# Sample keys and sequence 0's keys loaded in the prompt phase, output projection one sequence sooner

## Chip, cores and metric

The kernel runs on one core of a Trainium2 chip. The metric is the device time of the whole program in microseconds (us), the median over several runs. The engines are named as the profile names them: PE is TensorE's matmul (PEld its weight load), DVE is VectorE, ACT is ScalarE, POOL is GpSimd, SP is SyncE, which here only issues DMAs (SPq in the rows).

## What is computed

Two layers are run for two groups of tokens: one new stream of 1024 frames ("prompt") and 16 new frames for each of 8 running streams ("sample", 128 rows), which attend to 1024 cached keys and values each. Cut to the layer that the change touches:

```python
def _attn_gmlp_layer(x, cache_k, cache_v, ...):
    z = einsum('btd,de->bte', rmsnorm(x, norm_g), w_in)
    q, k, v, g_a, u_b, v_b, g_b = split(z)
    k_all, v_all = concat(cache_k, k), concat(cache_v, v)      # sample group only
    o = diff_attn(q, k_all, v_all, ...)                        # softmax(1) - lam * softmax(2), times v
    out_a = rmsnorm(o, subln_g) * 0.8 * silu(g_a)
    out_b = gelu(u_b) * spatial_gate(layernorm(gelu(v_b))) * silu(g_b)
    return x + einsum('bte,ed->btd', concat([out_a, out_b]), w_out)   # the output projection
```

Layer 1 is a convolution module (`w_in1`, a depthwise convolution of 31 taps, `w_out1`) on the normed result; then follows a last RMSNorm. Everything is float32 to the outside.

## The kernel before

**Precision and tiles.** A float32 product is made of three matmuls of split operands, high times high, high times low, low times high (`mm3`, L150). So every weight and every key that comes from memory goes through a split: a DMA into a tile named `raw`, a copy to the high part on ACT, a subtraction for the low part on DVE. Weights do this in `split_w` (L127). Keys are first transposed on PE into PSUM, and split from there (`kt_split`, L412). All of these `raw` tiles come from one pool of three buffers of 512 KB (`rawp`, L218): input weights, cached keys, the rows for the output projection and reloaded normed rows follow one another through the same three buffers.

Tokens come in 9 tiles of 128 rows: tiles 0 to 7 are the prompt, tile 8 is the sample group.

**Order of the work.** The program is written as one long sequence; a planner with a cost model then orders the instructions of each engine, an earlier place in the program being a higher priority, and hands out the buffers as it goes. An instruction whose inputs and buffer are there can so be put well before its place in the program. At run time each engine takes its instructions, and SP and POOL their DMAs, in the planned order.

**Prompt phase** (`phase_prompt`, L421). A loop over 32 steps n (4 heads, 8 query blocks) does attention, and beside it 45 gating "pieces" (`ga_piece`, `gm_piece`), three for every two steps. The last pieces belong to channel group 3. When all pieces are issued in program order (n = 30), `decode_begin` (L650) opens the pools of the decode phase, and the steps that are left, and the code after the loop, take from a list `ahead`: `setup` (loads the sample group's own keys and values, L673 to L678), and `keys_part(0, (i,))` for the four quarters of sequence 0's cached keys. A quarter is a `raw` load of two key tiles of 128, eight transposes in two groups of four, and the splits.

**Decode phase** (`phase_decode`, L712). A loop over the 8 sequences b; each issues `dscores(b)`, the keys of sequence b + 1 in two halves (`keys_part`), `dvalues(b - 1)` (cached values, loaded by POOL) and `dweights(b)`. Between them stand:

- `wl(b, j)`, which loads the next parts of `w_out0` as the table `WL` says: eight parts of 512 KB, four for each half of the output's columns;
- `prep(t)`: a `raw` tile (called cat below) is filled with the attention and the gating rows of tile t (`s_oa`, `s_ob`, two DMAs), transposed in two halves and split;
- `main(t)`: the output projection of tile t, 2 x 24 matmuls of 512 columns, the residual add, and the norm of layer 1. For t below `DIR` the normed rows are stored to `s_yn` and read back later; for the others they stay on chip.

Before, `prep` and `main` of tile b - 2 stand beside sequence b, so tiles 0 to 5 lie within the loop. After the loop come `dvalues(7)`, `prep(6)`, `dfinish` (norms the attention of the sample group and stores it to `s_oa`), `main(6)`, `prep(7)`, and then the hand-over to layer 1: `ynorm(t)` reloads normed rows through a `raw` buffer, and `yt` transposes and splits them; `main(7)`, `prep(8)` and `main(8)` stand among these. `prep(8)` reads what `dfinish` stored.

**Convolution phase** (`phase_conv`, L917). It starts with `split_w` of `w_in1`, through `raw` again; its first matmuls need token tiles 0 to 2 alone.

Of the kernel before, what the change touches and what calls it, by code (L numbers as in the profile page):

```python
# [11 lines left out]
F32 = mybir.dt.float32  # L12
# [7 lines left out]
P = 128  # L20
# [64 lines left out]
NSPLIT = True  # L85
MID = 1
ORDER = (0, 7, 1, 6, 2, 5, 3, 4)
DIR = 6
LOWG = ()
HP = 100  # L90
AHEAD = True
WL = ((0, 0, 2, 2), (2, 0, 2, 0))
VMID = False
TOEP = (2, 3, 4, 5)
TAIL = 1
# [7 lines left out]
class Builder:  # L103
# [317 lines left out]
    def phase_prompt(self):  # L421
        nc, tc, a = self.nc, self.tc, self.a
        w = a["w_in0"]
        with ExitStack() as st:
# [181 lines left out]
            def piece():  # L606
                nonlocal done
                if done < len(pieces):
                    pieces[done]()
                    done += 1  # L610

            for n, (h, qb) in enumerate((h, qb) for h in range(H) for qb in (order if h < H - 1 else LAST)):
                need = max(n + 2, round((n + 1) * LEAD)) if n < 8 else round((n + 1) * LEAD)
                need = min(need, len(pieces))
                while done < need - MID:
                    piece()
                if done == len(pieces) and not ahead and AHEAD:
                    while gates:
                        gate()
                    self.xstack.close()  # L620
                    ahead = self.decode_begin()
                elif ahead:
                    ahead.pop(0)()
                with tc.high_priority(offset=HP):
                    if n % 8 == 0:
                        head(h)
                    sc = scores(h, qb)
                    next(sc)
                    if VMID and pend is not None:
                        values(*pend)  # L630
                while done < need:
                    piece()
                with tc.high_priority(offset=HP):
                    new = next(sc)
                    if not VMID and pend is not None:
                        values(*pend)
                pend = new
# [9 lines left out]
            while ahead:  # L647
                ahead.pop(0)()

    def decode_begin(self):  # L650
        nc, tc, a = self.nc, self.tc, self.a
        dec = ExitStack()
        E = dec.enter_context
        vp = E(tc.tile_pool(name="vp", bufs=2, side="right", reuse_waits="tile"))
        ktp = E(tc.tile_pool(name="ktp", bufs=5, side="right", reuse_waits="tile"))
        ep = E(tc.tile_pool(name="ep", bufs=2, side="right", reuse_waits="tile"))
        ptc = E(tc.tile_pool(name="ptc", bufs=2, space=PSUM, side="right", reuse_waits="tile"))
        kTs = [ep.tile([P, H, P], F32R, name=f"kts{i}", bufs=1) for i in range(2)]
        vs = [ep.tile([P, 512], F32R, name=f"vs{i}", bufs=1) for i in range(2)]
        qs = [ep.tile([P, H, P], F32R, name=f"qs{i}", bufs=1) for i in range(2)]  # L660
        oacc = ep.tile([P, 512], F32, name="oacc", bufs=1)
        mk = ep.tile([P, C_SGN - C_FOLD], F32, name="mk", bufs=1)
        fold, own, place = mk[:, :64], mk[:, 64:576], mk[:, 576:]
        bs0 = ep.tile([P, 144], F32, name="bs0", bufs=1)
        seqs = [{} for _ in range(NB)]

        def setup():
            nc.sync.dma_start(out=mk, in_=a["cst"][:, C_FOLD:C_SGN])
            for c in range(2):
                nc.sync.dma_start(out=bs0[c * 64:(c + 1) * 64, :], in_=self.skew[:, :NQ, :144])  # L670
            nc.sync.dma_start(out=qs[0].bitcast(F32), in_=self.s_qh[:, :, T:])
            nc.sync.dma_start(out=qs[1].bitcast(F32), in_=self.s_ql[:, :, T:])
            raw = self.rawp.tile([P, 1024], F32, name="raw")  # L673
            nc.sync.dma_start(out=raw[:, :512], in_=self.k0s)
            nc.sync.dma_start(out=raw[:, 512:], in_=self.v0s)
            self.kt_split(raw[:, :512], kTs[0], kTs[1], ptc)
            nc.scalar.copy(vs[0], raw[:, 512:])
            nc.vector.tensor_tensor(vs[1], raw[:, 512:], vs[0].bitcast(F32), ALU.subtract)  # L678

        qz = [ep.tile([P, 2, 576], F32R, name=f"qz{i}", bufs=1) for i in range(2)]  # L680

        def keys_part(b, parts):
            if b >= NB:
                return
            K = seqs[b].setdefault("K", [])
            ck_ = a["cache_k0"][b].rearrange("(t p) h e -> p t (h e)", p=P)
            bq = slice(b * NQ, (b + 1) * NQ)
            if 0 in parts:
                if b < 2:
                    nc.gpsimd.memset(qz[b].bitcast(F32), 0.0)  # L690
                for i in range(2):
                    qv = qz[b % 2][:, i].rearrange("p (h s) -> p h s", s=144)
                    for c in range(2):
                        rs = slice(c * 64, (c + 1) * 64)
                        nc.gpsimd.tensor_copy(qv[rs, :, c * 64:c * 64 + NQ], qs[i][rs, :, bq].bitcast(F32))
            for i in parts:
                kr = self.rawp.tile([P, 1024], F32, name="raw").rearrange("p (t c) -> p t c", t=2)
                nc.sync.dma_start(out=kr, in_=ck_[:, 2 * i:2 * i + 2])
                KTh, KTl = [ktp.tile([P, H, 272 if i == 3 else 256], F32R, name=f"KT{n}x" if i == 3 else f"KT{n}",
                                     bufs=1 if i == 3 else 4) for n in "hl"]  # L700
                for j in range(2):
                    sl = slice(j * P, (j + 1) * P)
                    self.kt_split(kr[:, j], KTh[:, :, sl], KTl[:, :, sl], ptc)
                if i == 3:
                    nc.gpsimd.tensor_copy(KTh[:, :, 256:], kTs[0][:, :, bq].bitcast(F32))
                    nc.gpsimd.tensor_copy(KTl[:, :, 256:], kTs[1][:, :, bq].bitcast(F32))
                K.append((KTh, KTl))

        self.dec = dec, ep, vp, ptc, vs, oacc, fold, own, place, bs0, seqs, keys_part, qz
        return [setup] + [lambda i=i: keys_part(0, (i,)) for i in range(4)]  # L710

    def phase_decode(self):  # L712
# [114 lines left out]
        def prep(t):  # L827
            if t >= NT:
                return
            ts_ = slice(t * P, (t + 1) * P)  # L830
            cat = self.rawp.tile([P, D], F32, name="raw")
            nc.sync.dma_start(out=cat[:, :512], in_=self.s_oa[ts_, :])
            nc.sync.dma_start(out=cat[:, 512:], in_=self.s_ob[ts_, :])
            x = ck.tile([P, D], F32, name="xr", bufs=2)
            nc.sync.dma_start(out=x, in_=self.xrow(t))
            ch = ck.tile([P, 8, P], F32R, name="ch")
            cl = ck.tile([P, 8, P], F32R, name="cl")
            self.transpose_split(cat, [ch[:, :4], ch[:, 4:]], [cl[:, :4], cl[:, 4:]])
            st_[t] = (x, ch, cl)

        def main(t):
            x, ch, cl = st_[t]
            for i in range(2):
                ps = po_.tile([P, 512], F32, name="out")
                self.mm3(ps, [(ch[:, k], cl[:, k]) for k in range(8)], wb[i])
                xs = x[:, i * 512:(i + 1) * 512]
                nc.vector.tensor_tensor(xs, xs, ps, ALU.add)  # L847
            nc.gpsimd.dma_start(out=self.s_y1[t * P:(t + 1) * P, :], in_=x)
            xs = ck.tile([P, D], F32, name="yn")
            self.norm(xs, x, self.gb, NSPLIT and t < 8)  # L850
            if t < DIR:
                nc.gpsimd.dma_start(out=self.s_yn[t * P:(t + 1) * P, :], in_=xs)
            return xs
# [2 lines left out]
        nc.sync.dma_start(out=self.gb, in_=a["norm_g1"].partition_broadcast(P))  # L856
        for b in range(NB):
            dscores(b)
            if b > 1:
                prep(b - 2)  # L860
            keys_part(b + 1, (0, 1))
            wl(b, 0)
            if b > 0:
                dvalues(b - 1)
            wl(b, 1)
            if b > 1:
                main(b - 2)
            keys_part(b + 1, (2, 3))
            wl(b, 2)
            dweights(b)  # L870
            wl(b, 3)
        dvalues(NB - 1)
        prep(6)
        dfinish()
        m6 = main(6)
        prep(7)
        dec.close()
        self.pstack = ExitStack()
        self.ptr = self.pstack.enter_context(tc.tile_pool(name="ptr2", bufs=2, space=PSUM, side="right", reuse_waits="tile"))
# [16 lines left out]
            nc.sync.dma_start(out=yr, in_=self.s_yn[t * P:(t + 1) * P, :])  # L896
            yt(t, yr)

        ynorm(0)
        ynorm(1)  # L900
        yt(6, m6)
        m7 = main(7)
        prep(8)
        ynorm(2)
        ynorm(3)
        ynorm(4)
        ynorm(5)
        yt(7, m7)
        m8 = main(8)
        yt(8, m8)  # L910
# [305 lines left out]
```

## Time and profile before

| what | value |
|---|---|
| median of 3 runs | 1260.4 us (1257.78 to 1263.14) |
| the profiled execution | 1257.52 us, its span 1255.7 us |
| PE busy | 1186.4 us, 94% of the span |
| DVE, ACT, POOL busy | 830.0, 477.6, 365.6 us |
| granted clock, mean | 0.981 |
| DMA moved | 153.26 MB, 122 GB/s on the mean |
| first matmul of the output projection | 558.47 us |
| first matmul of the convolution phase | 770.33 us |

The profile's page gives the busy time of each engine, then the span in 40 slices, then the chain of work that ended last. Other views give stretches of time (busy time of each engine, granted clock, DMA rate) and the instructions of one engine in order of time: start, duration, engine, line, operation, output tile <- input tiles, and in brackets how long the engine had been idle and what ended that. A row with SPq is the issue of a DMA, not its transfer.

### The profile page before, as it was taken

To read this page: it belongs to the slowest core of one execution; us is meant where nothing else is said; L and a number is where in the kernel's file an instruction comes from. 1 tells how busy PE (TensorE), PEld (TensorE's weight loads), DVE (VectorE), ACT (ScalarE), POOL (GpSimd) and SP (SyncE) were. 2 spreads that over 40 slices of the span, in tenths; PEclk is the share of its full clock that TensorE was granted. 3 is DMA by queue.
4 is the path that set the end of the run, shared out by engine and by line. 5 is a ranking of instruction groups with operands and counts; after the bars stand their busy time and mean duration, and the time that the engine had idled before them with its cause. 6 is when DMAs were issued, how large, how long until landed. Compare 5 with 4: busy or idle time off the path is not lost.

```text
span 1255.7 us, 18564 instructions
## 1 busy us (share of the span) xinstructions
PE 1186.4 (94%) x6644; PEld 1078.1 (86%) x6644; DVE 830.0 (66%) x1695; ACT 477.6 (38%) x1090; POOL 365.6 (29%) x540
## 2 busy tenths in 40 slices
PE   6999999999989997889999999999999987999997
PEld 5878998999989887778888878999999987997886
DVE  5420225788687878686666535799999999267843
ACT  4431223445454545574544434211121212156421
POOL 2223223435353426222222221211424220033200
PEclk9999999999989999899999999999999997999999
DMA  8352444414141315685666545213231310212222
GB/s 295 106 164 70 152 150 128 119 55 116 39 124 42 112 41 163 225 287 203 223 213 232 185 150 184 66 40 88 72 108 49 122 59 24 67 35 101 101 96 73
DMA packets 121924, 153.26 MB, mean 122 GB/s; under 512 B 13577, under 2 KB 85281, under 8 KB 121824
## 3 DMA queue, kind: packets, MB, share of 16 engines
q1 hardware_dynamic: 107848, 108.21, 27.9%
q0 software_dynamic: 13840, 43.60, 10.2%
q8 instruction: 53, 0.87, 0.3%
q14 instruction: 39, 0.32, 0.1%
q10 hardware_dynamic: 144, 0.26, 0.1%
HBM read 116.22 MB, written 36.26 MB: 121 GB/s over the span
## 4 chain that ended last, share of the span: by engine, by line
PE 77%; DMA 8%; DVE 6%; ACT 4%; issue 2%; POOL 2%; SPq 0%; DVEq 0%; POOLq 0%; ACTq 0%
PE mm L155 50%; PE out L155 8%; PE py L1175 3%; PE S L155 3%; PE pa L589 2%; PE tr L416 2%; DMA vraw<-in_cache_v 2%; PE tr L165 2%; PE S L546 1%; PE S L547 1%; PE mm L787 1%; PE mm L761 1%; PE mm L786 1%; PE tr L584 1%; DVE wl L144 1%
## 5 line engine op out<-in xcount | busy, mean ns | idle before, releaser
L155 PE MATMUL mm<-yh,wh 128*128 128x384 f32 x576 | 196.5, 341 | 15.1 <-ACT sg L1024 12.6
L155 PE MATMUL mm<-yl,wh 128*128 128x384 f32 x576 | 195.2, 339 | 0.0
L155 PE MATMUL mm<-yh,wl 128*128 128x384 f32 x576 | 194.8, 339 | 0.0
L155 PE MATMUL mm<-wh,xh 128*128 128x384 f32 (+1 forms) x504 | 185.4, 369 | 1.3 <-DVE sg L469 0.6
L155 PE MATMUL mm<-wl,xh 128*128 128x384 f32 (+1 forms) x504 | 184.3, 366 | 1.7 <-DVE wl L144 1.7
L1151 DVE SCALAR_TENSOR_TENSOR acc<-u,cc,acc 128x1024 f32<-128x1024 f32 x145 | 185.4, 1279 | 0.4
L155 PE MATMUL mm<-wh,xl 128*128 128x384 f32 (+1 forms) x504 | 183.5, 364 | 0.0
L144 DVE TENSOR_TENSOR wl<-raw,wh 128x1024 fp32r<-128x1024 f32 (+1 forms) x72 | 91.3, 1274 | 91.6 <-ACT wh L143 91.0
L155 PEld LDWEIGHTS mm<-yh,wh 128*128 128x128 f32 x576 | 109.0, 189 | 15.9 <-ACT sg L1024 12.9
L155 PEld LDWEIGHTS mm<-yl,wh 128*128 128x128 f32 x576 | 109.1, 189 | 0.3
L155 PEld LDWEIGHTS mm<-yh,wl 128*128 128x128 f32 x576 | 109.0, 189 | 0.1
L155 PEld LDWEIGHTS mm<-wh,xh 128*128 128x128 f32 x504 | 95.5, 190 | 12.6 <-issue 1.1
L155 PEld LDWEIGHTS mm<-wl,xh 128*128 128x128 f32 x504 | 95.7, 190 | 11.7 <-DVE wl L144 3.2
L155 PEld LDWEIGHTS mm<-wh,xl 128*128 128x128 f32 x504 | 95.5, 190 | 8.8 <-DVE xl L168 0.3
L143 ACT CAST wh<-raw 128x1024 fp32r<-128x1024 f32 (+1 forms) x72 | 71.6, 1003 | 68.3 <-PE mm L155 30.6
L124 POOL TENSOR_TENSOR rr<-pw,mhalf 128x1 f32<-128x1 f32 x59 | 34.6, 586 | 169.2 <-DVE pw L123 160.8
L560 ACT ACTIVATE e<-S,nm 128x512 f32<-128x512 f32 (+5 forms) x96 | 55.2, 579 | 49.8 <-DVE nm L555 34.5
L1169 POOL TENSOR_TENSOR tw<-wx,same 128x640 f32<-128x640 f32 x24 | 37.4, 1560 | 80.3 <-PE py L1175 70.9
L552 DVE TENSOR_REDUCE nm<-S 128x1 f32<-128x512 f32 (+5 forms) x96 | 52.4, 550 | 12.1 <-PE S L547 11.4
L155 PE MATMUL out<-wh,cl 128*128 128x512 f32 x144 | 59.7, 415 | 0.0
L155 PE MATMUL out<-wh,ch 128*128 128x512 f32 x144 | 57.7, 401 | 1.7 <-DVE xr L847 1.2
L155 PE MATMUL mm<-wl,ch 128*128 128x512 f32 x144 | 56.9, 395 | 2.3 <-DVE wl L144 2.2
(287 smaller groups left out, 2572.7 us busy)
## 6 DMA issues: line engine op xcount, KB each, us to landing
raw<-in_cache_k SPq DMA_DIRECT2D x32, 512.0 KB, 4.5
vraw<-in_cache_v POOLq DMA_DIRECT2D x32, 512.0 KB, 5.2
raw<-in_w_in SPq DMA_DIRECT2D x24, 512.0 KB, 5.1
raw<-in_w_out SPq DMA_DIRECT2D x16, 512.0 KB, 4.1
raw<-in_w_in SPq DMA_DIRECT2D x32, 256.0 KB, 3.6
raw<-in_w_in SPq DMA_DIRECT2D x48, 128.0 KB, 3.2
s_y<-xr POOLq DMA_DIRECT2D x9, 512.0 KB, 5.5
x<-s_y SPq DMA_DIRECT2D x9, 512.0 KB, 4.1
```

The costliest lines, as they stand in the source:

```text
L124: m = nc.gpsimd.tensor_tensor(out, v[:, :w], self.mhalf[:, :w], ALU.pow)
L143: nc.scalar.copy(h[:, :ks * n], raw[:, :ks * n])
L144: (low or nc.vector).tensor_tensor(l[:, :ks * n], raw[:, :ks * n], h[:, :ks * n].bitcast(F32), ALU.subtract)
L155: m = self.nc.tensor.matmul(out, lhsT=x, rhs=y, start=(i == 0), stop=(i == n - 1))
L165: nc.tensor.transpose(ps[:, k * P:(k + 1) * P], src[:, kk * P:(kk + 1) * P], self.ident)
L416: nc.tensor.transpose(ps[:, h * P:(h + 1) * P], src[:, h * P:(h + 1) * P], self.ident)
L552: nc.vector.tensor_reduce(nm[:, j:j + 1], s[:, :n], AX.X, ALU.max, negate=True)
L560: nc.scalar.activation(e[:, j * n:(j + 1) * n], S[j][:, :n], AF.Exp, bias=nv, accum_out=zz[:, j:j + 1])
L589: nc.tensor.matmul(po, lhsT=wT[:, k * P:(k + 1) * P], rhs=hd["v"][:, k, :], start=(k == 0), stop=(k == qb))
L1151: tap = nc.vector.scalar_tensor_tensor(cv[:, :T] if k == CONV - 1 else acc, u[:, k:k + T], w1, acc, ALU.mult, ALU.add)
L1169: nc.gpsimd.tensor_tensor(tw.rearrange("p s (c f) -> p s c f", f=8), wx[:, g, :].rearrange("p (s f) -> p s f", f=8).unsqueeze(2).broadcast ...
L1175: nc.tensor.matmul(py, lhsT=tw[:, 4 - s, :], rhs=X[:, g, s:s + 176], start=(s == 0), stop=(s == 4))
```

## The change

Two things change in the order of the program; no arithmetic is added or removed.

1. `prefetch`, called in step n = 27 of the prompt loop, takes the three `raw` tiles for the sample keys and values and for the first two quarters of sequence 0's keys, and issues their four DMAs there. `setup` and `keys_part(0, ...)` use these tiles.
2. `prep(b - 1)` and `main(b - 1)` stand beside sequence b, so tiles 0 to 6 lie within the loop. Tile 6's normed rows now go through `s_yn` (`DIR` = 7). `WL` is changed so that all eight parts of `w_out0` are asked for before `main(0)`: two of them now stand between the two halves of sequence 1's keys, and none after sequence 2's first half. After the loop: `dvalues(7)`, `prep(7)`, `dfinish`, `main(7)`, `prep(8)`, seven reloads instead of six, `yt(7)`, `main(8)`, `yt(8)`.

```diff
-DIR = 6
+DIR = 7
+PRE = 27
-WL = ((0, 0, 2, 2), (2, 0, 2, 0))
+WL = ((0, 2, 2, 2), (2, 0, 0, 0))
...
+                if n == PRE:
+                    self.prefetch()
...
+    def keys_load(self, b, i):
+        kr = self.rawp.tile([P, 1024], F32, name="raw").rearrange("p (t c) -> p t c", t=2)
+        src = self.a["cache_k0"][b].rearrange("(t p) h e -> p t (h e)", p=P)
+        self.nc.sync.dma_start(out=kr, in_=src[:, 2 * i:2 * i + 2])
+        return kr
+
+    def prefetch(self):
+        raw = self.rawp.tile([P, 1024], F32, name="raw")
+        self.nc.sync.dma_start(out=raw[:, :512], in_=self.k0s)
+        self.nc.sync.dma_start(out=raw[:, 512:], in_=self.v0s)
+        self.fetched = raw, [self.keys_load(0, i) for i in range(2)]
...
-            raw = self.rawp.tile([P, 1024], F32, name="raw")
-            nc.sync.dma_start(out=raw[:, :512], in_=self.k0s)
-            nc.sync.dma_start(out=raw[:, 512:], in_=self.v0s)
+            raw = self.fetched[0]
...
-                kr = self.rawp.tile([P, 1024], F32, name="raw").rearrange("p (t c) -> p t c", t=2)
-                nc.sync.dma_start(out=kr, in_=ck_[:, 2 * i:2 * i + 2])
+                kr = self.fetched[1][i] if b == 0 and i < 2 else self.keys_load(b, i)
...
             dscores(b)
-            if b > 1:
-                prep(b - 2)
+            if b > 0:
+                prep(b - 1)
             keys_part(b + 1, (0, 1))
             wl(b, 0)
             if b > 0:
                 dvalues(b - 1)
             wl(b, 1)
-            if b > 1:
-                main(b - 2)
+            if b > 0:
+                main(b - 1)
             keys_part(b + 1, (2, 3))
             wl(b, 2)
             dweights(b)
             wl(b, 3)
         dvalues(NB - 1)
-        prep(6)
+        prep(7)
         dfinish()
-        m6 = main(6)
-        prep(7)
+        m7 = main(7)
+        prep(8)
...
-        ynorm(0)
-        ynorm(1)
-        yt(6, m6)
-        m7 = main(7)
-        prep(8)
-        ynorm(2)
-        ynorm(3)
-        ynorm(4)
-        ynorm(5)
+        for t in range(7):
+            ynorm(t)
         yt(7, m7)
         m8 = main(8)
         yt(8, m8)
```

More of the change, by code (lines that the diff above doesn't have):

```diff
@@ L685, in keys_part @@
             K = seqs[b].setdefault("K", [])
-            ck_ = a["cache_k0"][b].rearrange("(t p) h e -> p t (h e)", p=P)
             bq = slice(b * NQ, (b + 1) * NQ)
```

## The prediction

> **What bounds the kernel now.** I read the page first (busy times, the 40 slices, the chain), then the stretches of time around the decode phase, then SP's and PE's rows there.
>
> ```profile
> span 1255.7 us, 18564 instructions
> PE 1186.4 (94%) x6644; PEld 1078.1 (86%) x6644; DVE 830.0 (66%) x1695; ACT 477.6 (38%) x1090; POOL 365.6 (29%) x540
> ...
> PE   6999999999989997889999999999999987999997
> PEclk9999999999989999899999999999999997999999
> ...
> PE 77%; DMA 8%; DVE 6%; ACT 4%; issue 2%; POOL 2%; SPq 0%; DVEq 0%; POOLq 0%; ACTq 0%
> ```
>
> PE is busy for 94% of the span and carries 77% of the chain. No matmul is added or removed, so the time can only move by what changes in PE's idle time and in its clock. Slices 14 to 18 (440 to 565 us) and 23 to 25 (720 to 785) hold what the change can reach; there the stretches say (columns: length, busy us of PE, PEld, DVE, ACT, POOL with instructions, granted clock, DMA share, GB/s):
>
> ```profile
> 485.00:489.00 4.00, 1.10 (x6) 0.57 (x6) 3.53 (x12) 2.72 (x9) 4.00 (x7) 1.00 0.24 71
> 494.00:498.00 4.00, 0.72 (x4) 0.53 (x4) 3.20 (x7) 3.28 (x10) 3.95 (x5) 0.95 0.61 149
> 498.00:502.00 4.00, 3.94 (x17) 3.66 (x18) 3.85 (x12) 1.67 (x6) 1.14 (x3) 0.50 0.96 356
> 518.00:521.00 3.00, 0.64 (x6) 0.42 (x5) 1.92 (x3) 2.02 (x3) 2.25 (x6) 1.00 1.00 373
> 521.00:525.00 4.00, 2.73 (x13) 2.12 (x14) 3.45 (x8) 2.81 (x9) 0.00 (x0) 0.56 0.66 223
> 525.00:529.00 4.00, 4.00 (x23) 4.00 (x23) 2.46 (x5) 2.78 (x6) 0.00 (x0) 0.58 0.21 77
> 533.00:540.00 7.00, 6.54 (x42) 5.15 (x41) 5.98 (x11) 5.32 (x8) 2.11 (x8) 1.00 0.78 271
> 540.00:550.00 10.00, 8.67 (x61) 7.28 (x59) 8.44 (x13) 7.96 (x18) 2.22 (x5) 1.00 0.90 285
> 550.00:560.00 10.00, 8.47 (x49) 6.41 (x50) 8.87 (x13) 5.36 (x8) 1.61 (x3) 1.00 0.89 302
> 670.00:700.00 30.00, 30.00 (x189) 25.89 (x188) 19.80 (x30) 15.74 (x30) 9.03 (x13) 1.00 0.65 218
> 735.90:742.00 6.10, 4.86 (x21) 3.25 (x20) 3.06 (x8) 3.62 (x12) 1.97 (x3) 1.00 0.21 86
> 742.00:752.00 10.00, 10.00 (x57) 8.43 (x55) 4.04 (x8) 3.37 (x6) 3.13 (x3) 1.00 0.51 171
> 752.00:756.00 4.00, 2.26 (x13) 1.27 (x11) 2.58 (x5) 3.09 (x7) 1.15 (x2) 1.00 0.46 178
> ```
>
> Beside sequences with an output projection PE is full (30.00 of 30 us at 670): an output tile that leaves or enters such a stage only shifts work. Beside the first two sequences, 518 to 560, PE is idle for 2.36 + 1.27 + 0.46 + 1.33 + 1.53 = 6.95 us, and at 521 to 529 its clock is 0.56 to 0.58, which costs about 2.73 x 0.44 + 4 x 0.42 = 2.9 us more. So 9.8 us is all that can be won there. Behind the last sequence, 742 to 752, PE is full; what fills it is looked at below.
>
> **Part 1, the prefetch: nothing.** It moves four DMAs in the program, but the planner had them early already:
>
> ```profile
> 415.26 0.38 SPq L674 DMA_DIRECT2D raw<-out_k0s  x1
> 415.70 0.46 SPq L675 DMA_DIRECT2D raw<-out_v0s  x1
> 421.13 0.39 SPq L698 DMA_DIRECT2D raw<-in_cache_k  x1
> 436.65 0.39 SPq L698 DMA_DIRECT2D raw<-in_cache_k  x1
> ...
> 488.87 1.06 PE L416 MATMUL tr<-cst,raw 128*128 128x128 f32 x8 [2.90 <-issue]
> ```
>
> Sample keys and values and the two quarters of sequence 0 are issued at 415 to 437, in all three `raw` buffers, and first transposed at 488.87. PE's 2.90 us before that isn't theirs: the data has been there for some 45 us. By the code the new PSUM pool takes the place of the gating pieces' pool, and the last of these (DVE L469) ends at 488.8. That wait stays. The same three buffers are held, by the same tiles. From below: no gain, as nothing waits for these loads. From above: four issues of 0.4 us on SP ahead of the attention's own small loads, 1.7 us if those were late. I take 0; the cover is those 45 us.
>
> **Part 2, first sequences: a gain of about 5 us.** The unit that moves:
>
> ```profile
> 687.37 5.45 PE out L155 x24
> ...
> 741.73 1.03 PE L165 MATMUL tr<-cst,raw 128*128 128x128 f32 x8
> ```
>
> One tile is 2 x 5.45 + 1.03 = 11.9 us of PE. `main(0)` now stands beside sequence 1. Can it start sooner? It needs all of `w_out0` and its own cat tile through three `raw` buffers:
>
> ```profile
> 508.32 0.37 SPq L698 DMA_DIRECT2D raw<-in_cache_k  x1
> ...
> L137 SPq DMA_DIRECT2D raw<-in_w_out x8: 368/373/411, 512.8 to 547.1; - x8
> ...
> 518.01 1.05 ACT L143 CAST wh<-raw 128x1024 fp32r<-128x1024 f32 x1 [5.44 <-DMA raw<-in_w_out]
> 518.96 1.07 ACT L418 CAST KTh<-tr 128x512 fp32r<-128x512 f32 x2
> ...
> 520.97 1.78 PE L416 MATMUL tr<-cst,raw 128*128 128x128 f32 x8 [2.36 <-DVE KTl L419]
> ...
> 558.47 0.41 PE L155 MATMUL out<-wh,ch 128*128 128x512 f32 x1
> ```
>
> Between the first and the last weight part stand four key loads (the tables `WL` and `keys_part`): 11 steps in 34.3 us, 3.1 us a step. In the new order the first part takes the place of sequence 1's third key quarter, at 508.3; the last part is 12 steps on, at 545.5, only 1.6 us sooner than 547.1. But the first half's parts (5 steps, 523.8) and the cat tile (8 steps, 533.1) are there early: landed and split some 7 us later, the first 24 matmuls can run from about 540. They can fill the 1.33 + 1.53 us idle from 540 to 560: 3 us won. The second half starts about when it did.
>
> The other loss, 518 to 529, is a wait in ACT's queue: ACT stood 5.44 us for the first weight part, and the casts of sequence 1's second key quarter (518.96) were behind it; PE then had no keys to go on with. With the first part 4.5 us sooner, this wait shrinks by as much and may go: up to 3.6 us idle and 2.9 us of clock. What is late next is sequence 1's third and fourth key quarter, now two steps, 6.2 us, later, and the second weight part's cast stands ahead of theirs in ACT's queue: a wait of the same kind, down to -3 us (half of this one). No row shows the new order; I take +2, in the middle, as it is the same wait with another load in it. Together 5, ends 0 (3 - 3) and 9.5 (3 + 6.5), just under the 9.8 there is.
>
> **Part 3, behind the last sequence: a loss of about 8 us.** The tail's chain is `dfinish`, a store, a load, tile 8's transposes:
>
> ```profile
> 735.89 1.02 PE L793 MATMUL mm<-om,mk 128*128 128x512 f32 x2
> ...
> 743.08 0.60 POOL L812 DMA_DIRECT2D s_oa<-vraw  x1 [0.96 <-DVE vraw L810]
> ...
> 748.17 0.32 SPq L832 DMA_DIRECT2D raw<-s_oa  x1
> 748.60 11.79 SPq L896 DMA_DIRECT2D raw<-s_yn  x4
> 763.26 8.27 SPq L137 DMA_DIRECT2D raw<-in_w_in  x6
> ...
> raw<-s_oa SPq DMA_DIRECT2D x2, 256.0 KB, 3.2
> ```
>
> From sequence 7's last matmul (735.89) to the landing of tile 8's rows (748.17 + 3.2 = 751.4) pass 15.5 us, and SP's reloads of normed rows (748.60) are queued behind that load. Until 742 PE ends the tile in hand; then `main(7)` filled 742 to 752. With everything one tile sooner, the tile in hand is `main(7)`, and after 742 PE has only the transposes of two reloaded tiles and of tile 7, at most 3 x 1.03 = 3.1 us, for 9.4 us: 6.3 us idle. In return the 1.74 us idle of 752 to 756 shrinks, as the way is free for tile 8: 5 us net, 4.6 to 6.3.
>
> To this come the clock and the ring. After 2.9 and 3.28 us idle the clock was 0.50 at 498, after 3.6 us it was 0.56 to 0.58 for 8 us: 1.7 to 2.9 us lost each time. I take 2, and 0 as the lower end. [...]
>
> Tile 6 is now one store of 0.6 us on POOL, which nothing waits for, and one more reload in the ring ahead of `w_in1`, whose first load at 763.26 served matmuls that began at 770.33. With one step of 3.1 us as the upper end and 0 as the lower, as with less on PE the buffers come free sooner, I take 1. Sum of the tail: 5 + 2 + 1 = 8, ends 3 (3 us of idle if two more reloads get ahead of the waiting load and no slow clock) and 12.3 (6.3 + 2.9 + 3.1).
>
> **Sum.** 0 - 5 + 8 = +3 us. On the profiled execution, 1257.5 us (span 1255.7), that is 1260.5; this one lies 2.9 us under the median of 1260.4, so the forecast is 1263 us. The ends: -9.5 + 3 = -6.5, and 0 + 12.3 = +12.3. Half a per cent, 6.3 us, is about what a measurement of this kernel can tell from no change; the forecast is no change.
>
> **Rivals.**
>
> *Slower.* Sequence 1's late key quarters make PE stand a second time near 525 to 535. For it: ACT takes its casts in order, and from 518 to 525 the DMA share is 0.66 to 1.00. Against: by the pace the fourth quarter is issued at 517.6 and landed by 523, and PE wanted it only at 533. It decides from about 10 us of delay on. Price: the 3 us of fill are lost again, and the tail's 8 us stand alone: +8, 1268 us; with the tail's upper end +12, 1272 us.
>
> *Faster.* The stall of 518 to 529 goes altogether (-9.5), and the planner puts reloads three and four ahead of tile 8's load, so that the tail costs its lower end of 3: -6.5 us, 1254 us. For it: the 5.44 us wait hangs on one load that comes 4.5 us sooner. Against: DMA is as full, and before, the reloads were queued behind that load though their buffer was free.
>
> *It doesn't do what it says.* The planner holds `main(0)` back to where the last weight part lands, as now, and the tile only moves by name: no fill, but then tile 7 is also left over for the tail, and both terms go: 1260 us. This lies within no change.
>
> **Chances.** Forecast 0.45 and the empty change 0.10, both within 0.5%; slower 0.28 and faster 0.17 beyond it. The range, 1253 to 1272, runs from the faster case's price to the slower one's and leaves out about one in ten at each end.
>
> **What would show it.** Part 1: first key transposes again at about 489 after some 2.9 us of idle. Part 2: first projection matmul at about 540, less than 7 us idle from 518 to 560; ACT's wait for the first weight part below 2 us. Part 3: after the last sequence one idle stretch of 4 to 7 us ending in DMA `raw<-s_oa` or the transposes of tile 8, a clock below 0.7 behind it, and the stages between as full as now. It is wrong if PE stays full in the tail, or if sequence 1's scores wait for keys.

## The result, and the profile after

| | median | range | runs |
|---|---|---|---|
| before | 1261.13 us | 1257.78 to 1263.14 | 4 |
| after | 1275.43 us | 1271.37 to 1278.07 | 4 |

After to before is 1.0117, 95% interval 1.0087 to 1.0147: the change makes the kernel 14 us slower. The forecast was no change (1263 us); the range ended at 1272.

The two profiled executions are further apart than the medians: 1278.07 us (span 1276.3) is the slowest of its four runs, and 1257.52 us (span 1255.7) lies below all four of its own. A difference between the two traces so overstates the change by some 6 us, and sizes are taken from the medians of the experiments. The page of the changed kernel (span; busy time; PE and its clock in 40 slices):

```profile
span 1276.3 us, 18573 instructions
...
PE 1191.5 (93%) x6644; PEld 1082.4 (85%) x6644; DVE 832.4 (65%) x1695; ACT 477.2 (37%) x1090; POOL 362.9 (28%) x541
...
PE   6999999999899997899999968999999996999997
...
PEclk9999999999999998899999988999999997999999
```

PE does the same work. The row shows where it now stands: the 24th and 25th slice, 734 to 798 us, had 9 and 9 and have 6 and 8, with a clock of 8 in both. That is the tail. The stall of the head lies in slice 17, which has a clock of 8 before and after. Slice 16 (479 to 510 us) has 8 instead of 9, but that is scatter: PE's wait there, for an exponential of the prompt's attention, is 2.48 us before and 4.41 in this execution, and over the traces of all runs anything from under 0.6 to 4.41 us. Stretches of the changed kernel, columns as in the prediction:

```profile
518.00:521.00 3.00, 2.19 (x18) 1.89 (x16) 3.00 (x5) 0.92 (x2) 1.21 (x6) 1.00 0.97 331
521.00:525.00 4.00, 0.76 (x6) 0.42 (x4) 2.52 (x9) 3.12 (x10) 0.06 (x1) 0.92 1.03 409
525.00:529.00 4.00, 3.41 (x16) 3.44 (x17) 1.75 (x4) 2.02 (x4) 0.00 (x0) 0.50 0.54 196
540.00:550.00 10.00, 9.44 (x49) 7.02 (x49) 7.64 (x13) 7.00 (x15) 1.45 (x2) 1.00 0.75 236
550.00:560.00 10.00, 8.73 (x48) 7.82 (x47) 6.61 (x11) 3.79 (x7) 1.62 (x3) 0.83 0.88 309
670.00:700.00 30.00, 30.00 (x190) 25.86 (x188) 20.01 (x33) 15.21 (x30) 7.96 (x12) 1.00 0.65 234
749.59:756.00 6.41, 1.25 (x4) 0.38 (x2) 2.18 (x7) 2.69 (x11) 2.09 (x3) 0.77 0.20 82
756.00:762.00 6.00, 0.34 (x2) 0.34 (x3) 0.47 (x2) 0.99 (x1) 2.95 (x2) 0.50 0.40 143
762.00:770.00 8.00, 8.00 (x34) 6.58 (x33) 1.83 (x3) 2.24 (x4) 0.00 (x0) 0.70 0.41 155
```

The middle is as full as it was (30.00 of 30 at 670). The stall of the head has only moved: from 518 to 521, where PE was busy 0.64 of 3 us, to 521 to 525, 0.76 of 4, with the clock at 0.50 behind it. Over 518 to 560 together PE is idle for 6.64 us, and was for 6.94. In the tail PE does next to nothing for 11 us. The two instruction views name what it waits for. The head, on SP's queue and on PE:

```profile
509.38 0.37 SPq L138 DMA_DIRECT2D raw<-in_w_out  x1
512.95 0.39 SPq L138 DMA_DIRECT2D raw<-in_w_out  x1
513.89 0.38 SPq L656 DMA_DIRECT2D raw<-in_cache_k  x1
517.48 0.40 SPq L656 DMA_DIRECT2D raw<-in_cache_k  x1
...
520.51 1.27 PE L417 MATMUL tr<-cst,raw 128*128 128x128 f32 x8 [0.81 <-DVE KTl L420]
525.59 1.94 PE L417 MATMUL tr<-cst,raw 128*128 128x128 f32 x8 [3.81 <-DMA raw<-in_cache_k]
...
543.65 0.39 PE L156 MATMUL out<-wh,ch 128*128 128x512 f32 x1
```

Two weight parts now stand ahead of sequence 1's last two key quarters. The last quarter is issued at 517.48 and PE stands 3.81 us for it. The tail, on PE, POOL and SP:

```profile
744.10 0.39 PE L800 MATMUL mm<-vs,wt 128*128 128x512 f32 x1
749.59 1.02 PE L804 MATMUL mm<-om,mk 128*128 128x512 f32 x2
761.66 1.97 PE L166 MATMUL tr<-cst,raw 128*128 128x128 f32 x8 [10.82 <-DMA raw<-s_oa]
...
756.77 0.60 POOL L823 DMA_DIRECT2D s_oa<-vraw  x1 [0.96 <-DVE vraw L821]
...
759.15 0.32 SPq L843 DMA_DIRECT2D raw<-s_oa  x1
759.56 19.66 SPq L907 DMA_DIRECT2D raw<-s_yn  x6
...
781.78 0.32 SPq L907 DMA_DIRECT2D raw<-s_yn  x1
783.84 14.40 SPq L138 DMA_DIRECT2D raw<-in_w_in  x14
...
789.76 0.69 PE L156 MATMUL mm<-yh,wh 128*128 128x384 f32 x1 [1.11 <-ACT wh L144]
```

The second row is the last place matmul (L804), the same as the one at 735.89 before; the last row is the first convolution matmul. Between them lay 34.4 us and now lie 40.2, although a whole tile (11.9 us) less is left to do. All seven reloads (L907) stand behind tile 8's load and take SP from 759.56 to 782, since nearly each has to wait for one of the three `raw` buffers to come free (by the waits in the trace, SP stands 11.5 us for transposes and 6.2 us for projection matmuls). Ahead of them SP had stood 18.9 us at tile 8's load, for the store of `dfinish`. The first weights of the convolution are behind them. Before, four reloads stood behind that load, and the first two had been issued long ahead:

```profile
705.53 7.57 SPq L896 DMA_DIRECT2D raw<-s_yn  x2
```

From tile 8's load to the first `w_in1` load it was 748.17 to 763.26, 15.1 us; it is now 759.15 to 783.84, 24.7 us. Three reloads more, 9.6 us more.

### The profile page after: what moved, and what is told of

It is laid out like the page before. It is cut to its first block, busy times and chain, and to the rows that moved or that the text cites. A ratio compares the mean times of both kernels' runs of the same rounds, so it can differ in the third digit from the quotient of the medians.

```text
span 1276.3 us, 18573 instructions
## 1 busy us (share of the span) xinstructions
PE 1191.5 (93%) x6644; PEld 1082.4 (85%) x6644; DVE 832.4 (65%) x1695; ACT 477.2 (37%) x1090; POOL 362.9 (28%) x541
## 4 chain that ended last, share of the span: by engine, by line
PE 78%; DMA 8%; DVE 6%; issue 3%; ACT 3%; POOL 2%; SPq 0%; DVEq 0%; POOLq 0%; ACTq 0%
PE mm L156 52%; PE out L156 7%; PE py L1179 3%; PE S L156 3%; PE tr L417 2%; PE pa L590 2%; PE tr L166 1%; DMA vraw<-in_cache_v 1%; PE S L547 1%; PE mm L798 1%; DMA raw<-in_w_out 1%; PE S L548 1%; DMA raw<-in_w_in 1%; PE mm L772 1%; DVE wl L145 1%
## 5 line engine op out<-in xcount | busy, mean ns | idle before, releaser
L561 ACT ACTIVATE e<-S,nm 128x512 f32<-128x512 f32 (+5 forms) x96 | 55.1, 578 | 51.9 <-DVE nm L556 36.9
L790 DVE TENSOR_TENSOR vl<-vraw,vh 128x1024 fp32r<-128x1024 f32 x32 | 45.3, 1420 | 24.5 <-ACT vh L789 24.4
```

The lines of the kernel that those rows point to most:

```text
L561: nc.scalar.activation(e[:, j * n:(j + 1) * n], S[j][:, :n], AF.Exp, bias=nv, accum_out=zz[:, j:j + 1])
L790: (nc.vector if i in VDVE else nc.gpsimd).tensor_tensor(vl, vr, vh.bitcast(F32), ALU.subtract)
```

## The experiments

Each is given against the kernel before as run on the same chip (its median 1260.5 to 1261.4 us in all of them), with a 95% interval of the ratio. Where two changed kernels are compared, it is by their medians, mostly from different chips; as the 4 to 12 runs of a kernel spread over 4 to 12 us, a difference of less than some 3 us is not told from none (an estimate from these spreads).

**1. The prefetch alone.** All else as before.

```
 WL = ((0, 0, 2, 2), (2, 0, 2, 0))      # as before
 DIR = 6                                # as before
+                if n == PRE:
+                    self.prefetch()
```

> Part 1 alone: the prefetch, with the projection order, weight table and tail of before. Theory (the loads were early already, so the prefetch changes nothing): 1261 us, within 4 us of before, the first key transposes again at 489. Rival (the prefetch disturbs the prompt phase and carries part of the 14 us): 1265 us or more.

1258.81 us, ratio 0.9986 (0.9962 to 1.0010): nothing. DMA issues and matmuls stand in the same order as before; the planner had already put these loads where the new lines put them.

**2. The head alone.** New weight table and prefetch, tiles 0 to 5 beside sequences 1 to 6, the tail as before.

```
-            if b > 0:
+            if 0 < b < 7:
                 prep(b - 1)
...
         dvalues(NB - 1)
-        prep(7)
+        prep(6)
         dfinish()
-        m7 = main(7)
+        m6 = main(6)
...
```

> New first sequences, old tail: tiles 0 to 5 beside sequences 1 to 6, nothing beside sequence 7, tiles 6, 7 and 8 after it as before. Theory (the loss lies behind the last sequence, where no full tile of projection is left to cover the way from dfinish to tile 8): 1263 us, at most 4 us over before, no PE idle stretch over 3 us after the last sequence. Rival (the loss comes from the new order of keys and weights beside sequences 0 and 1): 1270 us or more.

1264.77 us, ratio 1.0026 (1.0010 to 1.0042). The head does not win 5 us, it loses 3.4. The time is within the theory's 4 us, but this is a loss where a gain was meant. Its trace has the changed kernel's stall, on PE:

```profile
524.28 1.41 PE L417 MATMUL tr<-cst,raw 128*128 128x128 f32 x8 [3.58 <-DMA raw<-in_cache_k]
```

**3. The tail alone.** Head as before but for the prefetch; tile 6 also stands beside sequence 7, and the new tail follows.

```
             if b > 1:
                 main(b - 2)
+            if b == 7:
+                prep(6)
+                main(6)
...
```

> Old first sequences, new tail: tiles 0 to 5 beside sequences 2 to 7 as before, tile 6 beside sequence 7 too, and after it the changed kernel's code. Theory of the tail: 1276 us, an idle stretch of some 10 us of PE that ends in tile 8's load, a clock near 0.65 behind it. Rival of the first sequences: 1261 us.

1266.72 us, ratio 1.0040 (1.0018 to 1.0061): 5.3 us, not the 15 expected. Stage 7 can't take a second tile: 96 projection matmuls were left behind the place matmul (97 before, 49 in the changed kernel), so the wait for tile 8 still had its cover. But all seven reloads stand behind tile 8's load: from it to the first `w_in1` load it is 25.6 us (15.1 before), and from the place matmul to the convolution 42.8 (34.4). Head and tail alone add up to 8.7 of 14.3 us; the rest needs both.

**4. The order of the reloads.** The changed kernel with `ynorm(0)` to `ynorm(3)` ahead of `prep(8)`.

```
         m7 = main(7)
-        prep(8)
...
-        for t in range(7):
+        for t in range(4):
+            ynorm(t)
+        prep(8)
+        for t in range(4, 7):
             ynorm(t)
```

> The changed kernel with four of the seven reloads of normed rows put ahead of tile 8's load in the program. Theory (the tail is as long as it is because all seven reloads stand behind that load in SP's queue): 1268 us, the idle stretch down from 10.8 us to about 7, and less idle among the transposes behind tile 8. Rival (only the length of the way from dfinish to tile 8 counts, reloads come in its shadow anyway): 1274 us or more.

1268.13 us, ratio 1.0053 (1.0032 to 1.0075): 7.3 us less than the changed kernel, the theory's answer. SP's queue and PE in this kernel:

```profile
742.77 0.32 SPq L906 DMA_DIRECT2D raw<-s_yn  x1
758.29 0.32 SPq L843 DMA_DIRECT2D raw<-s_oa  x1
...
760.81 5.35 SPq L906 DMA_DIRECT2D raw<-s_yn  x3
770.97 9.74 SPq L138 DMA_DIRECT2D raw<-in_w_in  x7
...
747.62 1.02 PE L804 MATMUL mm<-om,mk 128*128 128x512 f32 x2
756.33 1.94 PE L166 MATMUL tr<-cst,raw 128*128 128x128 f32 x8 [7.22 <-issue]
```

Three reloads are left behind tile 8's load, and the first `w_in1` load is issued 12.7 us after it, not 24.7. PE still stands 7.22 us, but the place matmul is 32.0 us ahead of the convolution instead of 40.2.

**5. The way out and back.** The changed kernel, with tile 8's attention rows written straight into the tile that `prep(8)` transposes.

```
+            cat = self.rawp.tile([P, D], F32, name="raw")
...
-                nc.vector.scalar_tensor_tensor(ga[:, hs], ...
+                nc.vector.scalar_tensor_tensor(cat[:, hs], ...
...
-            nc.gpsimd.dma_start(out=self.s_oa[T:, :], in_=ga)
+            st_["cat"] = cat
...
```

> The changed kernel, with tile 8's attention rows written by VectorE straight into the tile that its projection reads, so that their way out to s_oa and back is gone; all else, the order of the reloads too, as changed. In the changed kernel PE stood 10.82 us before tile 8's transposes (761.66, released by raw<-s_oa); of that the store was issued at 756.77 and the load landed at about 761.6, so some 5 us were the way out and back. Theory (the hole is the chain dfinish, store, load, with no matmul left beside it): the hole shrinks from 10.8 to about 6 us, the reloads of yn behind tile 8's load start some 2 us sooner, and the time goes to 1266 to 1270. Rival A (the hole does not matter, the reloads of yn and their evacuations set the end of the tail): 1273 to 1275. Rival B (the load is not what releases, another wait of the same length is behind it): the hole stays over 9 us, 1274 to 1276.

1270.87 us, ratio 1.0082 (1.0049 to 1.0114). The hole falls to 4.90 us, tile 8 begins 6.2 us after the place matmul instead of 12.1, and 36.9 us lie between place matmul and convolution:

```profile
742.43 1.02 PE L804 MATMUL mm<-om,mk 128*128 128x512 f32 x2
748.58 1.81 PE L166 MATMUL tr<-cst,raw 128*128 128x128 f32 x8 [4.90 <-DVE raw L823]
...
750.42 17.27 SPq L912 DMA_DIRECT2D raw<-s_yn  x4
...
769.43 0.32 SPq L912 DMA_DIRECT2D raw<-s_yn  x1
```

So 5.9 us off the start of tile 8 shorten the tail by 3.2. The hole is the theory's (about 6), the time just over its 1266 to 1270, and outside both rivals'. But the order of the reloads did not stay as changed, as the expectation has it: with tile 8's load gone from SP's queue, five of the seven are issued from 750.42 on, and the other two before 735. What the way out and back alone is worth, this run doesn't tell.

**6. The hole filled with work that no one needs.** The changed kernel with 40 matmuls into an unread PSUM tile, issued behind tile 7's projection.

```
+        with tc.issue_after(self.last_out):
+            ps = self.ptr.tile([P, 512], F32, name="tr")
+            for k in range(40):
+                nc.tensor.matmul(ps, lhsT=wb[0][k % 8][0][:, :P], rhs=wb[1][k % 8][0], ...)
```

> The changed kernel with 40 more 128x512 matmuls of already loaded weights into a PSUM tile that nothing reads, issued after tile 7's last projection matmul, so that TensorE is busy in most of the hole ahead of tile 8 (about 40 x 0.25 = 10 us of it). It leaves the hole's length as it is and takes away only that PE stands idle. Theory (part of the tail's loss is the granted clock, 0.63 in 750 to 762 and 0.70 in 762 to 770, where 8.0 us of busy time would have been some 5.6 at full clock): the clock in 762 to 770 is near 1.00, the tail is 2.5 to 4 us shorter, 1271 to 1273. Rival (behind the hole the reloads of yn set the pace, and the clock costs nothing): the clock rises, the time stays, 1274.5 to 1276. If the matmuls run past tile 8's load and hold it up: 1276 to 1280.

1275.61 us, ratio 1.0116 (1.0068 to 1.0165). PE's row of these matmuls, tile 8's transposes, and two stretches:

```profile
749.18 9.24 PE L890 MATMUL tr<-wh 128*128 128x512 f32 x40
760.30 1.10 PE L166 MATMUL tr<-cst,raw 128*128 128x128 f32 x8 [1.89 <-DMA raw<-s_oa]
...
748.09:760.00 11.91, 10.33 (x44) 7.88 (x42) 2.65 (x8) 3.69 (x11) 5.09 (x5) 1.00 0.27 98
760.00:768.00 8.00, 7.46 (x39) 5.89 (x40) 2.58 (x4) 2.15 (x4) 0.00 (x0) 1.00 0.56 196
```

The clock is 1.00 where it was 0.50 to 0.77 and 0.70, and the medians differ by 0.2 us, as the rival has it. With four runs that spread over 10 us they alone don't exclude the theory's 2.5 to 4 us; but from place matmul to convolution it takes 38.7 us instead of 40.2, so in these two traces the slow clock was worth at most 1.5 us.

**7. Keys ahead of weights.** The changed kernel with the first two weight parts behind all four key quarters of sequence 1.

```
-WL = ((0, 2, 2, 2), (2, 0, 0, 0))
+WL = ((0, 0, 2, 2), (4, 0, 0, 0))
```

> The changed kernel with the projection's first two weight parts issued behind all four key quarters of sequence 1 instead of ahead of the last two. In the changed kernel sequence 1's third quarter was issued at 517.48 and PE stood 3.81 us for it at 525.59, with the clock at 0.50 in 525 to 530. Theory (the stall is only exchanged: the weights come later by about the 8 us of the quarters, PE then stands for the first projection matmuls, which have nothing else beside them): the key wait goes, the first projection matmul comes at 546 to 552 instead of 543.6, the time stays within 3 us, 1273 to 1278. Rival (the late quarters are the head's loss, the weights have slack): the key wait and its slow clock go, the time falls by 4 to 6 us, 1269 to 1271.

1270.78 us, ratio 1.0073 (1.0044 to 1.0103): 4.7 us less, the rival's answer. (The quarter issued at 517.48 in the changed kernel is the fourth; the third, as the expectation calls it, was issued at 513.89.) SP's queue and PE:

```profile
510.33 0.39 SPq L656 DMA_DIRECT2D raw<-in_cache_k  x1
511.82 0.38 SPq L138 DMA_DIRECT2D raw<-in_w_out  x1
...
520.99 1.31 PE L417 MATMUL tr<-cst,raw 128*128 128x128 f32 x8 [3.38 <-DVE KTl L420]
524.00 1.12 PE L417 MATMUL tr<-cst,raw 128*128 128x128 f32 x4 [1.70 <-DVE KTl L420]
...
536.72 0.47 PE L156 MATMUL out<-wh,ch 128*128 128x512 f32 x1
```

This run's first key transposes are at 486.87, 2.0 us sooner than the changed kernel's; counted from there, the last key quarter is issued 5 us sooner. The old stall is back (released by the keys' split, as before the change), and the projection, too, starts 5 us sooner than with the weights first: the weights had slack, the keys had none.

**8. The planner's priority.** The changed kernel with `dvalues(7)` and `dfinish` under a higher priority.

> The changed kernel with only the planner's priority of the last sequence's values and of what finishes them raised, so that its place matmul (749.59 in the changed kernel, with its operand om ready at 745.2) is not put behind 23 of tile 7's projection matmuls; these stay behind it to fill the wait for tile 8. Theory (the hole is long because tile 7's projection was spent ahead of the place matmul): the place matmul comes some 4 us sooner, the hole falls from 10.8 to 5 to 7 us, 1269 to 1272. Rival (the matmuls only change places, and the reloads of yn, started by tile 8's load, set the end): the load comes 4 us sooner too, so the reloads do, and the time falls by the same 4 us, with the hole filled; told apart by PE's idle time between 780 and 790, which then stays at 5 us. Third: the raised priority puts the last sequence's transposes side by side where PE waits for ScalarE's copies of them, and gives back 2 to 4 us, 1274 to 1277.

1276.00 us, ratio 1.0122 (1.0083 to 1.0162). It told nothing: the place matmul stood at 750.04, the hole was 10.92 us, and no matmul ahead of the convolution had changed places. It is another run of the changed kernel.

**9. The filler held back.** The changed kernel, with the second half of tile 7's projection (24 matmuls) behind the place matmul.

```
+            self.placed = nc.tensor.matmul(po, ...)
...
+                with tc.issue_after(self.placed.ins) if (t, i) == (7, 1) else ExitStack():
                     self.mm3(ps, [(ch[:, k], cl[:, k]) for k in range(8)], wb[i])
```

> The changed kernel with the second half of tile 7's projection (24 of its 48 matmuls, some 5.9 us) held behind the last place matmul, where the planner had put nearly all 48 ahead of it. The raised priority of the run before did not move one of them (place matmul 750.04, hole 10.92), so that this now asks the question for the first time. Theory (the hole is long because tile 7's projection was spent ahead of the place matmul, whose operand om was ready at 745.2 while it ran at 749.59): the place matmul comes 3 to 4.4 us sooner, the load of tile 8 and the reloads behind it as much sooner, the 24 matmuls lie in the hole, which shows 4 to 6 us instead of 10.8, and the time falls from 1275.4 to 1271 to 1272.5. Rival (the matmuls only cross the place matmul, and TensorE stands ahead of it for om as long as it stood behind): the place matmul comes less than 1 us sooner, 1274 to 1276.

1273.99 us, ratio 1.0109 (1.0084 to 1.0135): between the two, and not settled by the time. The hole is halved (5.01 us), and place matmul to convolution takes 40.0 us, as without it. The trace is on the theory's side: the place matmul (749.38) is 1.2 us behind the last values matmul instead of 5.5, and counted from the first key transposes (491.48 here, 488.83 in the changed kernel) it comes 2.9 us sooner.

**10. Keys first and the filler held back.** The same pair of questions again, on the kernel of experiment 7.

> The changed kernel with the keys first and half of tile 7's projection held behind the last place matmul; the tail's loads in the changed order. Against the keys first alone (1270.8). Theory (idle time in the hole costs nothing by itself, the chain from the place matmul to the convolution stays at 40 us, and the hold is worth only what the place matmul comes sooner by, about 2 to 3 us): 1267.5 to 1269.5, with the hole near 5 us and the chain at 40. Rival A (the hole's idle time is the loss, half of it filled is some 5.8 us): 1264 to 1266, chain near 34. Rival B (the hold is worth nothing): 1270 to 1272.

1263.98 us, ratio 1.0037 (1.0020 to 1.0054), 6.8 us under experiment 7. PE and SP of this kernel:

```profile
738.35 1.13 PE L804 MATMUL mm<-om,mk 128*128 128x512 f32 x2 [0.78 <-DVE om L802]
750.00 1.97 PE L166 MATMUL tr<-cst,raw 128*128 128x128 f32 x8 [5.05 <-DMA raw<-s_oa]
...
777.65 0.69 PE L156 MATMUL mm<-yh,wh 128*128 128x384 f32 x1 [1.05 <-ACT wh L144]
...
747.13 0.32 SPq L843 DMA_DIRECT2D raw<-s_oa  x1
747.55 19.89 SPq L908 DMA_DIRECT2D raw<-s_yn  x6
```

The time is rival A's, the mechanism is the theory's: the chain keeps its length (39.3 us, against 40.6 in experiment 7) though the hole is half filled, and the place matmul, now right behind its operand, stands at 738.35 instead of 743.77 (6.1 us sooner, counted from the first key transposes, 487.57 and 486.87). The theory had the size too small: nearly all of the 5.5 us of held matmuls came off the start of the chain. The two pairs give 1.4 and 6.8 us by the medians, and 1.0 and 4.5 us by the ratios to each chip's kernel before; why they differ stays open.

**11. Repairs together.** Three kernels on the changed one: keys first and the reload order; these and the direct write; these and the held half as well.

> The changed kernel with two repairs, weights behind sequence 1's keys and reloads of yn 0 to 3 ahead of tile 8's load. Theory (the late keys and the queue of reloads behind tile 8's load are each a loss of their own): 1275.4 less 4.7 less 7.3 = 1263.4, so 1262 to 1265, and the other two repairs make up the 6 us down to 1257.3. Rival (these two are all that counts, the wait for tile 8's load is covered once the reloads are ahead of it): 1257 to 1260.

1262.40 us, ratio 1.0015 (0.9997 to 1.0033), within the theory's 1262 to 1265.

> The changed kernel with three repairs, keys first, reloads of yn 0 to 3 ahead, tile 8's attention rows written straight into the projection's tile; without the hold of tile 7's projection. Theory (the hold is worth what the place matmul comes sooner by, some 2 to 3 us, since it starts the chain that ends in the convolution): 1259 to 1261. Rival (without the way out and back the chain is short enough for the reloads to cover it, and the hold is worth nothing): 1256.5 to 1258.5.

1260.61 us, ratio 1.0007 (0.9988 to 1.0025), the theory's answer.

> The changed kernel with the repairs together: weights behind sequence 1's keys, reloads of yn 0 to 3 ahead of tile 8's load, tile 8's attention rows written straight into the tile that the projection reads, and half of tile 7's projection held behind the last place matmul. One by one the first three took 4.7, 7.3 and 4.6 us off 1275.4; the last two overlap in the same hole. Theory (these are the change's whole loss, and moving a tile sooner is worth nothing more): 1258 to 1262, as before. Rival A (under the losses lies the gain that was meant, some 5 us for the idle time that the earlier tile fills): 1254 to 1257. Rival B (the tail has a loss left, because the reloads' evacuations are slower than TensorE however early they load): 1263 to 1266.

1257.30 us, ratio 0.9968 (0.9951 to 0.9984): a little better than expected, and the one version that beats the kernel before, by 4 us. This is less than the half per cent that the prediction called measurable, but the interval excludes no change. The direct write and the held half are no part of the change, and neither was run on the kernel before, so the 4 us are not shown to be won by moving a tile. Its stretch from place matmul to convolution and SP's reloads in it:

```profile
741.24:771.70 30.46, 25.66 (x122) 20.03 (x123) 14.33 (x25) 13.45 (x27) 4.53 (x4) 0.94 0.47 149
...
740.71 17.88 SPq L912 DMA_DIRECT2D raw<-s_yn  x5
```

From place matmul to convolution it takes 30.5 us, PE idle for 4.8 of them; the last five reloads are issued from 740.71 on (the other two before 730), and none waits behind a load of tile 8.

**12. The head alone, repaired.** The kernel of experiment 2 with the keys first; and with the direct write too.

> The head of the change alone (prefetch, earlier weights, tiles 0 to 5 beside sequences 1 to 6, the tail as before), with the weight parts now behind all four key quarters of sequence 1, as in the run of the changed kernel that this order made 4.7 us shorter. The head alone was 3.4 us slower than before (1264.8). Theory (the head's loss is the late key quarters and nothing else): 1259 to 1261.5, no slower than before. Rival (the head loses elsewhere, for example by a tile beside sequence 1 for which the stages have no idle time, and the 4.7 us came by way of the tail): 1263 to 1265.

1259.64 us, ratio 0.9997 (0.9978 to 1.0017): the 3.4 us are gone, and nothing is won.

> The head alone with the weights behind the keys and the tail as before, and tile 8's attention rows written straight into the tile that the projection reads. In the run of the head alone PE still stood 2.93 us for tile 8's load (756.88) and 1.43 us ahead of it. Theory (the load's way out and back is still the last wait of the old tail): 2 to 4 us under the same head without it, 1256 to 1259. Rival (tile 7's projection covers that wait as soon as the reloads are ahead of it): the same as that head, within 1 us, 1259 to 1261.5.

1258.87 us, ratio 0.9990 (0.9971 to 1.0010): 0.8 us under the same head without it, as the rival had it, though the time also lies in the theory's range; so small a difference is within either interval.

## Why the prediction was wrong

The sum was 0 - 5 + 8 = +3. Measured: 0 for the prefetch (experiment 1), +3.4 for the head (2), and what is left of the 14.3, +10.9, for the tail behind that head. The head missed by 8 us and the tail by 3; both errors had the same sign. The rival *Slower* had the right mechanism for the head, a second wait for sequence 1's keys, but priced it as the fill lost and no more, with 1272 us as its end.

**Part 1 was right.** The same four loads are issued at 417 to 437 as before, the first key transposes come at 488.83 after 2.93 us of idle (before 488.87 and 2.90), and alone the prefetch changes nothing.

**Part 2, the failed step: "a wait of the same kind, down to -3 us ... I take +2, in the middle".** Each part of the mechanism was there. ACT's wait for the first weight part went, the last key quarter was issued at 517.48 (517.6 by the pace), and the projection began at 543.65 (540). What was wrong stands in the rival *Slower*: "landed by 523, and PE wanted it only at 533". It was transposed at 525.59, PE having been idle for it since 521.8, so sequence 1's scores waited for keys, which the prediction names as a sign that it is wrong. The landing was some 2.5 us late, with the DMA share at 1.03; the need was more than 10 us too late in my text. No row shown supported 533: the prediction quoted the issue of sequence 1's third quarter (508.32) but not its last transposes, which in the trace of before run at 528.80, just ahead of the sequence's first `cf` matmul at 530.55. So the condition of that rival, 10 us of delay, was set far too high: 6 us did it. Experiments 7 and 12 size it: keys first takes 4.7 us off the changed kernel and 5.1 off the head alone.

The fill of 3 us did not show either. With the keys first, the head alone is no different from before (experiment 12: 0.9997, from 2.8 us less to 2.1 us more), and PE's idle time at 540 to 560 in the changed kernel, 0.56 + 1.27 us, is only 1.0 us less than before.

**Part 3, the failed step: "one more reload in the ring ... I take 1".** The place was right, and of the signs named for it two held: one idle stretch that ended in `raw<-s_oa`, and a slow clock behind it (0.70 in 762 to 770, at the named bound). The third did not: the stretch is 10.82 us long, not 4 to 7. The sizes were wrong in all three terms. Two rows of the kernel before, behind its place matmul (735.89), bear on the second:

```profile
736.35 0.80 PE L155 MATMUL out<-wh,cl 128*128 128x512 f32 x1
738.38 0.47 PE L155 MATMUL out<-wh,ch 128*128 128x512 f32 x1 [1.24 <-DVE xr L847]
```

- *The ring, 1.* Behind tile 8's load stand not one reload more but three: tile 6's, and the two that the planner had issued at 705.53 before. At 3.2 us each that is the 9.6 us by which the way to the first `w_in1` load got longer; the order of the reloads alone is worth 7.3 us (experiment 4). The prediction saw that reloads are queued behind that load, and in the rival *Faster* asked whether two more might get ahead of it, but never whether those that were ahead would stay there.
- *The idle time, 5 net.* 10.82 us instead of 6.3 gross. The prediction has PE end "the tile in hand" until 742, and `main(7)` fill the time from there. But in its own trace the tile in hand, 6, ended at the place matmul: 23 of its matmuls run between the last values matmul (730.40) and the place matmul, one behind it (736.35), and `main(7)` begins at 738.38; with tile 8's these are the 97 behind the place matmul. The changed kernel has the same 23 and one, of tile 7, and behind them only tile 8. So PE is out of work from 750.8 on, and the two reloads whose transposes were to fill part of the time are not there yet. As far as experiments 6 and 10 show, the hole itself costs nothing. What costs is that matmuls which could run beside the chain (store, load, reloads, convolution weights) run ahead of it: the place matmul that starts it has its operand `om` ready at 745.2 and runs at 749.59. Before, it came 4.4 us late, too, but two whole tiles were left to run beside the chain. Holding 24 of the matmuls back took 1.4 us off in one pair and 6.8 in the other (experiments 9 and 10).
- *The clock, 2.* No effect seen (experiment 6: 0.2 us in the medians, at most 1.5 us in the traces). The lower figure of its range, 1.7, is shown by no run: 3.94 us busy at 0.50 are 2.0 us. The clock fell as expected (0.50 in 756 to 762), but on a stretch in which PE was ahead of the reloads anyway (it stands for one again at 786.96). The error was to price a slow clock where PE does not set the end.

The interaction that head and tail alone don't show (5.6 of 14.3 us) fits the counts in the traces, but no run isolates it. The head alone has as much of the projection left behind the last values matmul as the changed kernel (73 and 72 matmuls; 120 before and in the tail alone). But there 72 of the 73 stand behind the place matmul, which comes 1.2 us behind the last values matmul instead of 5.5, two reloads are issued at 709.97, long ahead of tile 8's load, and from the place matmul to the convolution it takes 30.8 us instead of 40.2. The tail alone has the queue of reloads, but 96 matmuls to run beside it. Only the changed kernel has both: seven reloads behind tile 8's load, and 49 matmuls beside them.

## What to carry to other kernels

When a load moves ahead in a shared queue, read the slack of what it passes from the row that uses that load (the transposes), not from a later stage: here six microseconds of delay met none. When work is moved forward out of a tail, list what the tail's wait was covered by, and what each queue will then hold behind the instruction that waits; the order of seven reloads around one load was worth 7.3 us, and the tile moved sooner won nothing that could be measured. An idle stretch, and a slow clock behind it, are not a price until an experiment fills them.

## What the runs showed of the hardware

The clock fell with PE's idle time as forecast (0.50 after 3.81 us, and 0.50 within the 10.82 us), but no cost of it showed in the tail: 12 us in the hole at 1.00 instead of 0.50 to 0.77, and the 8 us behind it at 1.00 instead of 0.70, changed the median by 0.2 us (four runs each). A 512 KB key quarter needed 8 us from issue to use where the DMA share was 0.97 to 1.03. And single executions of one kernel spread over 4 to 12 us, so that these two profiled ones showed 20.6 us of difference where the medians have 14.3.
